# Gate projections moved behind the projections, and six PSUM banks for the first mixer, in a two-layer hybrid decoder on one core

## The chip, the cores and the metric

The kernel runs on one core of a Trainium2 chip. The metric is device time in microseconds for one execution, the median of three runs. The core's engines are TensorE (PE, with its weight loads PEld), VectorE (DVE), ScalarE (ACT), GpSimd (POOL) and SyncE (SP), which here only issues DMAs.

## The reference

2048 positions of width 1024 pass through a gated short-convolution mixer and then a stick-breaking attention of 8 heads of width 64, all in float32. Keys and values come from one shared projection.

```python
h = _rmsnorm(x, norm_a)                                   # layer 0: mixer
b_gate, c_gate, xin, g = jnp.split(h @ w_in, 4, axis=-1)
y = b_gate * _causal_depthwise_conv(c_gate * xin, w_conv)
x = x + (y * jax.nn.silu(g)) @ w_out
k, v = jnp.split(_rmsnorm(x, norm_kv) @ w_kv, 2, axis=-1) # shared
q, g = jnp.split(_rmsnorm(x, norm_b) @ w_in_b, 2, axis=-1)  # layer 1
z = jnp.einsum("bhqd,bhkd->bhqk", q, k) * HEAD_DIM ** -0.5
rev = lax.cumsum(where(mask, log_sigmoid(-z), 0.0), axis=3, reverse=True)
o = einsum("bhqk,bhkd->bhqd", exp(where(mask, z + rev, -inf)), v)
x = x + (o * jax.nn.silu(g)) @ w_out_b
return _rmsnorm(x, norm_f)
```

## The kernel before

Everything is held transposed: 128 channels on the partitions, positions along the free axis. The 2048 positions are cut into four chunks of 512 (in reversed order, so that the reversed cumulative sum becomes a forward scan). Each float32 product is made of three TensorE products: both operands are split into a high part in fp32r and a remainder (`split`: ACT makes the high part, DVE or POOL the remainder), and `mm3` (lines 202 to 214) runs high x high, high x low, low x high. A block of 128 output channels over 1024 input channels is therefore 24 matmuls of 512 columns. Weights are split once, kept in DRAM with their two halves, and loaded by SP for every later use, 1 MB for each block, into four buffers (`whl`).

The work for one chunk `c`:

- `mixer_in` (line 282): for each of 8 channel blocks the four parts C, X, B and G of the input projection, 24 matmuls each, followed by convolution and gating on DVE and ACT; the result goes to `y_d` in DRAM. Chunks 0 and 1 run together and share each weight load; chunks 2 and 3 run alone.
- `proj_out` (line 372): the mixer's output projection (8 blocks, tiles `po`), the residual, the norm, and the split normed tiles `xn`, kept in SBUF in `kept[c]`.
- `proj_k`, `proj_q`, `proj_v`, `proj_g`: 4 blocks each. The gate block (`proj_g`, tiles `pg` and `sgb`) ends with a sigmoid on ACT, a product on DVE and a write to `sg_d`. `proj_first` holds the output projection and the first k, q and v block, `proj_rest` the others and all four gate blocks.
- `attention` (line 466) for one head: for each chunk of keys up to `c`, four tiles of scores `z`, two sigmoids on ACT, a scan on DVE (line 501), a product (line 505), then transposes on TensorE (`wt`), a split (`wth` on ACT, `wtl` on DVE), and the product with the values into `av`. A head ends with the addition into `ot` (line 531).
- `out_b` (line 567): attention output times gate (`gated`), the last output projection (8 blocks of 12 matmuls, tiles `pob`), residual, sum of squares; `out_stat` and `out_norm` finish the last norm. For chunk 3 `out_b_last` does this in two parts, three quarters before the last pair of heads is done and the rest at the end.

PSUM has eight banks of one 128x512 tile: two each for `lin` (all projections), `z` and `wt`, one for `av`, one for `st` (norm statistics). A projection's bank is free again when DVE or ACT has read it.

What is issued next is decided in two steps. The program is made of generators that yield their cost, and `merge` (line 672) runs several of them side by side, always the one that has the smallest share of its stated total done; the totals are counted in `LIN`, one block of 24 matmuls (`TA` a mixer chunk, `TF` and `TR` the first and the remaining projections, `TO` an output projection). A scheduler then places the instructions on each engine's queue in that order of priority. Within a queue the order is fixed. SP's queue is one: a load stands behind an earlier write that still waits for its data.

The merges before are, in order: the mixer of chunks 0 and 1; the projections of chunk 0 with part of chunk 2's mixer; the projections of chunk 1 with more of that and attention of chunk 0; the rest of chunk 2's mixer with attention of chunk 1; the projections of chunk 2 with chunk 3's mixer and attention; the rest of that mixer with attention of chunk 2; `proj_first(3)` with the rest of attention of chunk 2; then these:

```python
fill = chain(proj_rest(3), gated_in(0), out_b(0, range(KD)), out_stat(0), gated_in(1), ...
merge((fill, TR + 3 * TO), (heads(0, 3, 3), 0.75 * ta(3)))
tail = chain(gated_in(3, range(3)), take(last, NB * 9 * MM), out_norm(2), until(last, -1.0))
merge((tail, 72 * MM), (heads(3, 4, 3), 0.25 * ta(3), S7))
```

In these last two the filler is paced: every third matmul of a projection is ordered behind the ninth last product of attention with the values.

Of the kernel before, what the change touches and what calls it, by code (L numbers as in the profile page):

```python
# [8 lines left out]
F32 = mybir.dt.float32  # L9
# [5 lines left out]
P = 128  # L15
# [3 lines left out]
KD = D // P  # L19
# [26 lines left out]
def kernel(  # L46
# [47 lines left out]
    k_d = [[dram.tile([P, CH], F32, name=f"k_d_{c}_{h}") for h in range(NH)] for c in range(NCH)]  # L94
    q_d = [[dram.tile([P, 2, CH], F32, name=f"q_d_{c}_{h}") for h in range(NH // 2)] for c in range(NCH)]
    v_d = [dram.tile([P, 4, NH, 2, 64], F32, name=f"v_d_{c}") for c in range(NCH)]
    sg_d = [[dram.tile([P, CH], F32, name=f"sg_d_{c}_{h}") for h in range(NH // 2)] for c in range(NCH)]
    og_d = [[dram.tile([P, CH], F32, name=f"og_d_{c}_{h}") for h in range(NH // 2)] for c in range(NCH)]

# [177 lines left out]
        return hc  # L277

    h = {}
    late_acc, late = {}, {}  # L280

    def mixer_in(cs):
# [3 lines left out]
        for cb in range(KD):  # L286
            wts = {}
            for c in cs:
# [5 lines left out]
                def gate(g, i):  # L294
                    if c not in h:
                        if c == 0:
                            load_first = lambda: wts.update({g: load_w(w_src(i), (g, cb), f"{g}{cb}_{cs[0]}")})
                            h[c], late_acc[c] = norm_x_late(c, load_first)
                        else:
                            h[c], xs = norm_x_late(c)  # L300
                            late_acc[c] = rstd(squares(c, xs), f"h{c}")
                    if g not in wts:
                        wts[g] = load_w(w_src(i), (g, cb), f"{g}{cb}_{cs[0]}")
                    if c == cb == 0 and g in "BG":

                        ps = psum.tile([P, CH], F32, name=f"p{g}_{nm}", tag="z", bufs=NZ)
                    else:
                        ps = lin(f"p{g}_{nm}")
                    yield from mm3(ps, wts[g], h[c])
                    return ps  # L310
# [61 lines left out]
    def proj_out(c):  # L372
# [23 lines left out]
        for k in range(KD):  # L396
            xn = act_tile(f"xn_{c}", k)
            nc.vector.tensor_mul(x1[k], x1[k], pb)
            split(xn[:, 0, :], xn[:, 1, :], x1[k], nc.gpsimd if k in XNL else nc.vector)
            kept[c].append(xn)  # L400
        yield YP[c] * 24 * MM

    def proj_k(c, kb):
# [49 lines left out]
    def proj_rest(c):  # L453
        yield from proj_k(c, 1)
        yield from proj_q(c, 1)
        yield from proj_v(c, 1)
        yield from proj_v(c, 2)
        yield from proj_v(c, 3)
        for i in (2, 3):
            yield from proj_k(c, i)  # L460
            yield from proj_q(c, i)
        for i in range(4):
            yield from proj_g(c, i)

# [198 lines left out]
    def take(g, cost):  # L663

        while cost > 0:
# [3 lines left out]
            cost -= r  # L669
            yield r  # L670

    def merge(*streams):

        anchors.clear()
# [8 lines left out]

    UD, UF = 3300.0, 5300.0
    LIN = 24 * MM
    TA, TF, TR, TO = 32 * LIN, 11 * LIN, 13 * LIN, 4 * LIN

    def ta(c):
        return 8 * UD + 8 * c * UF
# [4 lines left out]
    def heads(lo, hi, c):  # L694
        for hb in range(lo, hi):
# [5 lines left out]
            else:  # L701
                nc.sync.dma_start(out=og_d[c][hb], in_=ot)

    TP = TF + TR
    m01 = mixer_in((0, 1))
    run(take(m01, TA / 4))
    merge((m01, 1.75 * TA), (chain(iter((DLY,)), stats_x(2), stats_x(3), fold_gains()), 18.0 + DLY))
# [5 lines left out]
    m3 = mixer_in((3,))  # L713
    merge((chain(proj_first(2), proj_rest(2)), TP), (take(m3, F3 * TA), F3 * TA), (a1, (1 - F2) * ta(1), S3))
    merge((m3, (1 - F3) * TA), (take(a2, F4 * ta(2)), F4 * ta(2), S4))
    merge((proj_first(3), TF), (a2, (1 - F4) * ta(2)))
    fine[:] = [GRY, True]
    lo, hi = range(0, NB), range(NB, KD)
    fill = chain(proj_rest(3), gated_in(0), out_b(0, range(KD)), out_stat(0), gated_in(1),
                 out_b(1, lo), out_norm(0), out_b(1, hi), gated_in(2), out_stat(1),  # L720
                 out_b(2, lo), out_norm(1), out_b(2, hi), out_stat(2))
    merge((fill, TR + 3 * TO), (heads(0, 3, 3), 0.75 * ta(3)))
    tail = chain(gated_in(3, range(3)), take(last, NB * 9 * MM), out_norm(2), until(last, -1.0))
    merge((tail, 72 * MM), (heads(3, 4, 3), 0.25 * ta(3), S7))
    run(last)


# [25 lines left out]
```

## Time and profile before

| | |
|---|---|
| median of 3 runs | 1899.47 us (1899.46 to 1902.62) |
| profiled execution | 1899.87 us, span 1898.2 us |
| PE busy | 1787.5 us (94%), 8312 matmuls |
| DVE busy | 1264.4 us (67%) |
| ACT busy | 771.9 us (41%) |
| POOL busy | 433.3 us (23%) |
| mean granted TensorE clock | 0.975 |
| DMA | 443.65 MB, mean 234 GB/s |

Busy time is an average over stages with different limits, and a matmul that waits counts as busy. So the profile is read by stage: windows of the span with each engine's busy time, and the times at which heads end.

### The profile page before, as it was taken

To read this page: it belongs to the slowest core of one execution; us is meant where nothing else is said; L and a number is where in the kernel's file an instruction comes from. 1 tells how busy PE (TensorE), PEld (TensorE's weight loads), DVE (VectorE), ACT (ScalarE), POOL (GpSimd) and SP (SyncE) were. 2 spreads that over 40 slices of the span, in tenths; PEclk is the share of its full clock that TensorE was granted. 3 is DMA by queue.
4 is the path that set the end of the run, shared out by engine and by line. 5 is a ranking of instruction groups with operands and counts; after the bars stand their busy time and mean duration, and the time that the engine had idled before them with its cause. 6 is when DMAs were issued, how large, how long until landed. Compare 5 with 4: busy or idle time off the path is not lost.

```text
span 1898.2 us, 24937 instructions
## 1 busy us (share of the span) xinstructions
PE 1787.5 (94%) x8312; PEld 1453.6 (77%) x8312; DVE 1264.4 (67%) x1927; ACT 771.9 (41%) x1497; POOL 433.3 (23%) x822
## 2 busy tenths in 40 slices
PE   7999999999999999999999999999989999888784
PEld 5777888888888878888888888888857777766563
DVE  7766533564133273538886437787996989999996
ACT  6323211231122132325453324444564666566553
POOL 5100000101011031202222102223231323654651
PEclk9999999999999999999999999999989999999797
DMA  9989855697888778776767776656838565777751
GB/s 291 313 293 311 301 154 163 198 355 252 292 270 283 225 261 266 243 266 204 266 214 264 236 253 202 202 191 197 253 104 266 178 195 175 251 252 252 236 170 50
DMA packets 233871, 443.65 MB, mean 234 GB/s; under 512 B 17936, under 2 KB 132624, under 8 KB 209168
## 3 DMA queue, kind: packets, MB, share of 16 engines
q1 hardware_dynamic: 173664, 383.31, 60.1%
q10 hardware_dynamic: 59920, 58.74, 10.7%
q8 instruction: 66, 1.08, 0.2%
q14 instruction: 61, 0.50, 0.1%
q0 software_dynamic: 160, 0.02, 0.1%
HBM read 314.34 MB, written 127.66 MB: 233 GB/s over the span
## 4 chain that ended last, share of the span: by engine, by line
PE 68%; DVE 17%; DMA 6%; issue 5%; ACT 2%; POOL 1%; SPq 0%; ACTq 0%; POOLq 0%; DVEq 0%
PE pX L208 8%; PE pB L208 7%; PE po L208 7%; PE pC L208 7%; PE pG L208 7%; DVE R L501 5%; PE pv L208 4%; PE pk L208 4%; PE wt L513 4%; PE pq L208 4%; PE pg L208 4%; DVE w L505 3%; PE av L523 3%; DVE wtl L175 2%; PE av L522 2%
## 5 line engine op out<-in xcount | busy, mean ns | idle before, releaser
L501 DVE TENSOR_TENSOR_SCAN R<-R,R,ones 128x512 f32<-128x512 f32 x192 | 259.2, 1352 | 23.5 <-ACT R L490 23.2
L490 ACT ACTIVATE R<-z 128x512 f32<-128x512 f32 (+1 forms) x320 | 174.2, 545 | 171.5 <-DVE R L501 80.5
L175 DVE TENSOR_TENSOR wtl<-wt,wth 128x512 fp32r<-128x512 f32 (+1 forms) x320 | 186.2, 600 | 60.7 <-ACT wth L174 60.1
L174 ACT CAST wth<-wt 128x512 fp32r<-128x512 f32 (+1 forms) x320 | 160.6, 528 | 153.2 <-PE wt L513 134.1
L505 DVE TENSOR_TENSOR w<-w,R 128x512 f32<-128x512 f32 (+1 forms) x320 | 209.2, 661 | 16.1 <-POOL R L500 0.5
L208 PE MATMUL pC<-h,whl_C 128*128 128x512 f32 x768 | 193.3, 401 | 14.4 <-ACT whl_C L174 8.2
L208 PE MATMUL pX<-h,whl_X 128*128 128x512 f32 x768 | 188.4, 395 | 5.9 <-DVE cv L350 5.9
L208 PE MATMUL po<-y,whl_o 128*128 128x512 f32 x768 | 187.8, 392 | 0.0
L208 PE MATMUL pB<-h,whl_B 128*128 128x512 f32 x768 | 185.5, 391 | 0.0
L208 PE MATMUL pG<-h,whl_G 128*128 128x512 f32 x768 | 185.0, 391 | 0.0
L500 POOL COPY R<-R 128x1 f32<-128x1 f32 x192 | 103.9, 541 | 349.3 <-DVE R L501 302.2
L208 PEld LDWEIGHTS pC<-h,whl_C 128*128 128x128 f32 x768 | 146.4, 193 | 48.5 <-ACT whl_C L174 8.2
L513 PE MATMUL wt<-ident,w 128*128 128x128 f32 x1088 | 178.5, 279 | 4.3 <-DVE w L505 3.2
L492 ACT ACTIVATE w<-z 128x512 f32<-128x512 f32 (+1 forms) x320 | 171.9, 542 | 6.5 <-PE wt L513 6.5
L208 PEld LDWEIGHTS pX<-h,whl_X 128*128 128x128 f32 x768 | 143.9, 189 | 37.3 <-issue 3.6
L523 PE MATMUL av<-wtl,vv 128*128 128x512 f32 (+1 forms) x320 | 128.9, 405 | 41.5 <-DVE wtl L175 40.1
L208 PEld LDWEIGHTS po<-y,whl_o 128*128 128x128 f32 x768 | 143.1, 188 | 30.2 <-ACT y L174 0.4
L208 PEld LDWEIGHTS pB<-h,whl_B 128*128 128x128 f32 x768 | 143.4, 188 | 29.6
L208 PEld LDWEIGHTS pG<-h,whl_G 128*128 128x128 f32 x768 | 143.3, 188 | 29.7 <-DVE sgb L443 0.2
L513 PEld LDWEIGHTS wt<-ident,w 128*128 128x128 f32 x1088 | 139.7, 144 | 33.1 <-issue 4.2
L501 DVE TENSOR_TENSOR_SCAN R<-R,ones 128x512 f32<-128x512 f32 (+3 forms) x128 | 116.8, 918 | 36.0 <-POOL R L496 32.5
L487 PE MATMUL z<-kt,q 128*128 128x512 f32 (+1 forms) x320 | 129.9, 408 | 7.3 <-ACT w L492 7.1
(170 smaller groups left out, 2676.9 us busy)
## 6 DMA issues: line engine op xcount, KB each, us to landing
whl_o<-sw_o SPq DMA_DIRECT2D x24, 1024.0 KB, 6.1
kt<-k_d ACTq DMA_DIRECT2D x80, 256.0 KB, 4.0
vv<-v_d ACTq DMA_DIRECT2D x80, 256.0 KB, 4.2
whl_C<-sw_C SPq DMA_DIRECT2D x16, 1024.0 KB, 5.9
whl_X<-sw_X SPq DMA_DIRECT2D x16, 1024.0 KB, 5.4
whl_B<-sw_B SPq DMA_DIRECT2D x16, 1024.0 KB, 5.5
whl_G<-sw_G SPq DMA_DIRECT2D x16, 1024.0 KB, 5.3
whl_k<-sw_kv SPq DMA_DIRECT2D x16, 1024.0 KB, 5.6
```

The lines of the kernel that those rows point to most:

```text
L174: nc.scalar.copy(hi, src)
L175: eng.tensor_sub(lo, src, hi.bitcast(F32))
L208: ins = nc.tensor.matmul(ps, w[:, k, :], a[k][:, m, :], start=n == 0, stop=n == 3 * kt - 1)
L487: nc.tensor.matmul(ps[:, lom:CH], q2[:, 0, qi * P:(qi + 1) * P], kt[:, lom:CH], start=True, stop=False)
L490: nc.scalar.activation(R[:, lo + 1:CH + 1], ps[:, lo:CH], AF.Sigmoid, scale=-0.125)
L492: nc.scalar.activation(w[:, lo:CH], ps[:, lo:CH], AF.Sigmoid, scale=0.125)
L500: nc.gpsimd.tensor_copy(R[:, 0:1], carry[qi])
L501: nc.vector.tensor_tensor_scan(out=R[:, lo + 1:CH + 1], data0=R[:, lo + 1:CH + 1], data1=ones[:, 0:1].to_broadcast([P, CH - lo]), initial= ...
L505: nc.vector.tensor_mul(w[:, lo:CH], w[:, lo:CH], R[:, lo:CH])
L513: nc.tensor.transpose(wt[:, qi * P:(qi + 1) * P], ws[qi][:, kb * P:(kb + 1) * P], ident)
L522: nc.tensor.matmul(av[:, 0:n], vs, wh[:, 0:n], start=first, stop=False)
L523: ins = nc.tensor.matmul(av[:, 0:n], vs, wl[:, 0:n], start=False, stop=final)
```

## The change

The gate projections are taken out of `proj_rest`. Chunk 2's run beside chunk 3's output projection and attention of chunk 2; chunk 3's, and then those of chunks 0 and 1, run as filler beside attention of chunk 3, chunk 1's in turn with chunk 0's last output projection. For chunks 0 and 1 the normed tiles `xn` are by then gone from SBUF, so they are written to DRAM (`xn_d`, 8 tiles of 512 KB per chunk) and loaded again as `xa`. The last output projection of chunk 2 moves from the filler of the first three pairs of heads to that of the last pair. The mixer's results for chunks 0 and 1 go in turn to the two banks each of `lin`, `z` and `wt`, in place of `lin` with two exceptions.

```diff
+    xn_d = [[dram.tile([P, 2, CH], F32, name=f"xn_d_{c}_{k}") for k in range(KD)] for c in range(NCH - 2)]
...
+    turn = [0]
...
-                    if c == cb == 0 and g in "BG":
-
-                        ps = psum.tile([P, CH], F32, name=f"p{g}_{nm}", tag="z", bufs=NZ)
+                    if len(cs) > 1:
+
+                        tag, bufs = (("lin", NLIN), ("z", NZ), ("wt", NWT))[turn[0] % 3]
+                        turn[0] += 1
+                        ps = psum.tile([P, CH], F32, name=f"p{g}_{nm}", tag=tag, bufs=bufs)
...
             kept[c].append(xn)
+            if c < NCH - 2:
+                nc.sync.dma_start(out=xn_d[c][k], in_=xn.bitcast(F32))
...
         for i in (2, 3):
             yield from proj_k(c, i)
             yield from proj_q(c, i)
+
+    def proj_gate(c, again=True):
+        if again:
+
+            kept[c] = [act_tile(f"xa_{c}", k) for k in range(KD)]
+            for k in range(KD):
+                nc.sync.dma_start(out=kept[c][k].bitcast(F32), in_=xn_d[c][k])
         for i in range(4):
             yield from proj_g(c, i)
...
+    def zipped(*gens):
+
+        live = list(gens)
+        while live:
+            for g in list(live):
+                r = next(g, None)
+                if r is None:
+                    live.remove(g)
+                else:
+                    yield r
...
-    TA, TF, TR, TO = 32 * LIN, 11 * LIN, 13 * LIN, 4 * LIN
+    TA, TF, TR, TG, TO = 32 * LIN, 11 * LIN, 13 * LIN, 4 * LIN, 4 * LIN
...
-    TP = TF + TR
+    TP = TF + TR - TG
...
-    merge((proj_first(3), TF), (a2, (1 - F4) * ta(2)))
+
+    merge((proj_first(3), TF), (a2, (1 - F4) * ta(2)), (proj_gate(2, False), TG))
...
-    fill = chain(proj_rest(3), gated_in(0), out_b(0, range(KD)), out_stat(0), gated_in(1),
-                 out_b(1, lo), out_norm(0), out_b(1, hi), gated_in(2), out_stat(1),
-                 out_b(2, lo), out_norm(1), out_b(2, hi), out_stat(2))
-    merge((fill, TR + 3 * TO), (heads(0, 3, 3), 0.75 * ta(3)))
-    tail = chain(gated_in(3, range(3)), take(last, NB * 9 * MM), out_norm(2), until(last, -1.0))
-    merge((tail, 72 * MM), (heads(3, 4, 3), 0.25 * ta(3), S7))
+    first_out = chain(gated_in(0), out_b(0, range(KD)), out_stat(0))
+    fill = chain(proj_rest(3), proj_gate(3, False), proj_gate(0), zipped(first_out, proj_gate(1)), gated_in(1),
+                 out_b(1, lo), out_norm(0), out_b(1, hi), gated_in(2), out_stat(1))
+    merge((fill, TR + 2 * TG + 2 * TO), (heads(0, 3, 3), 0.75 * ta(3)))
+    tail = chain(out_b(2, lo), out_norm(1), out_b(2, hi), out_stat(2),
+                 gated_in(3, range(3)), take(last, NB * 9 * MM), out_norm(2), until(last, -1.0))
+    merge((tail, TO + 72 * MM), (heads(3, 4, 3), 0.25 * ta(3), S7))
```

Three places show how the instructions move. In the rows below the first letters name the tile, the next figure its block, and the last number only tells tiles apart; `x3` is three such instructions.

On TensorE, at the end of chunk 0's projections, the last gate block (`pg_3`) stood ahead of chunk 1's output projection (`po_0`). Before:

```order
L208 MATMUL pg_3_4293<-xn_5_3526,whl_gg_3_4291 128x512 x3
L208 MATMUL pg_3_4293<-xn_6_3530,whl_gg_3_4291 128x512 x3
L208 MATMUL pg_3_4293<-xn_7_3534,whl_gg_3_4291 128x512 x3
L513 MATMUL wt_1_0_2_4837<-ident,w_1_0_2_4737 128x128
L208 MATMUL po_0_4365<-y_0_4322,whl_o_0_4363 128x512
```

Now the last query block (`pq_3`) stands there:

```order
L209 MATMUL pq_3_4193<-xn_5_3579,whl_q_3_4191 128x512 x3
L209 MATMUL pq_3_4193<-xn_6_3584,whl_q_3_4191 128x512 x3
L209 MATMUL pq_3_4193<-xn_7_3589,whl_q_3_4191 128x512 x3
L535 MATMUL av_1_4565<-wth_1_0_1_4750,vv_1_0_4568 128x256
L536 MATMUL av_1_4565<-wtl_1_0_1_4751,vv_1_0_4568 128x256
L535 MATMUL av_1_4565<-wth_1_0_0_4758,vv_1_0_4568 128x256
L209 MATMUL po_0_4265<-y_0_4222,whl_o_0_4263 128x512
```

The four gate blocks are gone from this place, and likewise at the end of the projections of chunks 1 and 2.

On SP's queue, where chunk 0's normed tiles are made, the weights of the first key block (`whl_k_0`) and of the mixer's next blocks were followed by loads of the residual (`x_1`). Before:

```order
L194 DMA whl_k_0_3694<-sw_kv_1297 128x2048
L389 DMA x_1_0_4390<-in_xT_dram 128x512
L389 DMA x_1_1_4519<-in_xT_dram 128x512
L389 DMA x_1_2_4603<-in_xT_dram 128x512
L194 DMA whl_C_2_3728<-sw_C_0_980 128x2048
```

Now:

```order
L406 DMA xn_d_0_203<-xn_0_3554 128x1024
L393 DMA x_1_0_4290<-in_xT_dram 128x512
L406 DMA xn_d_3_206<-xn_3_3569 128x1024
L393 DMA x_1_1_4419<-in_xT_dram 128x512
L195 DMA whl_k_0_3778<-sw_kv_1313 128x2048
L406 DMA xn_d_1_204<-xn_1_3559 128x1024
L406 DMA xn_d_6_209<-xn_6_3584 128x1024
L406 DMA xn_d_2_205<-xn_2_3564 128x1024
L406 DMA xn_d_4_207<-xn_4_3574 128x1024
L406 DMA xn_d_5_208<-xn_5_3579 128x1024
```

The writes of `xn` stand among the weight loads, two of them ahead of the first key block's, and each waits for its tile's split.

On TensorE in chunk 3's third head (head 2, tiles `z_2`, `wt_2`, `av_2`), the filler between attention's matmuls was the last of chunk 3's gates and then chunk 0's output projection. Now chunk 0's gates on the reloaded tiles `xa` stand there:

```order
L209 MATMUL pg_3_14193<-xn_7_12474,whl_gg_3_14191 128x512 x3
L209 MATMUL pg_0_14298<-xa_0_14280,whl_gg_0_14296 128x512
L500 MATMUL z_2_0_0_14270<-kt_2_0_14266,q_3_2_13877 128x512
L501 MATMUL z_2_0_0_14270<-kt_2_0_14266,q_3_2_13877 128x512
L209 MATMUL pg_0_14298<-xa_0_14280,whl_gg_0_14296 128x512
L535 MATMUL av_2_13880<-wth_2_2_3_14067,vv_2_2_14008 128x512
L209 MATMUL pg_0_14298<-xa_0_14280,whl_gg_0_14296 128x512
L209 MATMUL pg_0_14298<-xa_1_14281,whl_gg_0_14296 128x512 x3
L209 MATMUL pg_0_14298<-xa_2_14282,whl_gg_0_14296 128x512 x3
L536 MATMUL av_2_13880<-wtl_2_2_3_14068,vv_2_2_14008 128x512
```

Eight gate blocks of 24 matmuls that ran in the projections of chunks 0 and 1 now lie between the matmuls of these heads.

## The prediction

> **What bounds the kernel now.** I read the page's 40 slices first, to see which engine is full where. Each digit is the busy share of 47 us, in tenths.
>
> ```profile
> PE   7999999999999999999999999999989999888784
> DVE  7766533564133273538886437787996989999996
> PEclk9999999999999999999999999999989999999797
> DMA  9989855697888778776767776656838565777751
> ```
>
> TensorE is full for two thirds of the span while VectorE is half idle. From slice 33 on it is the other way round: VectorE reads 9 throughout, and TensorE drops to 8 and 7. So a TensorE job is worth its full length early and perhaps little late. The windows by stage give the sizes (the columns are named in the first row).
>
> ```profile
> core 0: us, PE busy (x) PEld busy (x) DVE busy (x) ACT busy (x) POOL busy (x), PEclk, DMA share, GB/s
> 69.00:237.00 168.00, 162.15 (x697) 133.01 (x698) 101.73 (x163) 43.94 (x65) 6.70 (x15) 0.97 0.87 296
> 237.00:386.00 149.00, 149.00 (x659) 123.35 (x658) 64.58 (x82) 33.05 (x43) 9.06 (x16) 1.00 0.58 179
> 386.00:588.00 202.00, 201.28 (x912) 166.31 (x911) 79.92 (x139) 46.57 (x84) 15.24 (x35) 1.00 0.86 290
> 588.00:842.00 254.00, 251.41 (x1184) 208.94 (x1183) 111.50 (x196) 69.24 (x155) 41.32 (x116) 1.00 0.77 255
> 842.00:1144.00 302.00, 300.76 (x1465) 249.96 (x1464) 198.54 (x315) 123.80 (x258) 55.69 (x152) 1.00 0.72 240
> 1144.00:1313.00 169.00, 169.00 (x845) 141.08 (x843) 134.44 (x182) 81.71 (x169) 46.32 (x100) 1.00 0.60 192
> 1313.00:1475.00 162.00, 147.63 (x699) 115.88 (x697) 135.14 (x207) 85.67 (x178) 43.11 (x94) 0.96 0.66 213
> 1475.00:1614.00 139.00, 132.98 (x666) 108.77 (x667) 126.84 (x165) 85.93 (x173) 44.72 (x87) 0.98 0.57 180
> 1614.00:1831.00 217.00, 179.70 (x816) 136.72 (x815) 207.52 (x299) 128.18 (x255) 120.66 (x158) 0.92 0.73 236
> 1831.00:1867.00 36.00, 28.68 (x130) 21.57 (x129) 30.82 (x41) 19.26 (x37) 13.38 (x16) 0.91 0.36 114
> ```
>
> From 386 to 1313 TensorE is busy 922 of 927 us: every matmul taken out there ends the stage earlier. From 1614 to 1867 VectorE is busy 238 of 253 us.
>
> A busy TensorE also counts waiting inside a matmul, so I count its work instead: one block of 24 matmuls of 512 columns, and one transpose.
>
> ```profile
> 565.21 5.44 PE pg L208 x24
> ```
> ```profile
> 1461.99 0.82 PE L513 MATMUL wt<-ident,w 128*128 128x128 f32 x6
> 1462.56 0.48 PE L487 MATMUL z<-kt,q 128*128 128x512 f32 x1
> 1462.88 0.40 PE L488 MATMUL z<-kt,q 128*128 128x512 f32 x1
> ```
>
> A block takes 5.44 us, so a matmul 0.227 us; six transposes and one z make 0.89 us start to start, so a transpose 0.11 us. Adding TensorE's order at these prices gives 1697 us of work, the same before and after: the change only moves it. The span is 1898.2 us; about 200 us of it TensorE works at nothing. The change can only win by shrinking those 200.
>
> To see where the late ones lie I cut the trace at the ends of attention heads, the last addition into `ot` (start us, us, engine and line).
>
> ```profile
> 1313.20 0.69 DVE L531 TENSOR_TENSOR ot<-ot,av 64x512 f32<-64x512 f32 x1
> ...
> 1475.03 0.69 DVE L531 TENSOR_TENSOR ot<-ot,av 64x512 f32<-64x512 f32 x1
> ...
> 1614.18 0.67 DVE L531 TENSOR_TENSOR ot<-ot,av 64x512 f32<-64x512 f32 x1
> ...
> 1831.54 0.67 DVE L531 TENSOR_TENSOR ot<-ot,av 64x512 f32<-64x512 f32 x1
> ...
> 1867.07 0.69 DVE L531 TENSOR_TENSOR ot<-ot,av 64x512 f32<-64x512 f32 x1 [1.21 <-ACT ot L530]
> ```
>
> **Term 1, gates out of the full stages.** Four gate blocks leave each of chunks 0, 1 and 2: 3 x 4 x 5.44 = 65.3 us. In TensorE's order the work ahead of the end of the twentieth head (1313.20) falls from 1260 to 1190 us, 70.5: the other 5 us are blocks that the new merge weights put later. The stages they leave are TensorE's, so all of it counts: **-70.5 us**. With each gate block go a sigmoid of 0.60 us and a product of 0.69.
>
> ```profile
> L443 DVE TENSOR_TENSOR sgb<-sgb,pg 128x512 f32<-128x512 f32 x16 | 11.0, 685 | 44.8 <-ACT sgb L442 44.8
> ...
> L442 ACT ACTIVATE sgb<-pg 128x512 f32<-128x512 f32 x16 | 9.6, 598 | 41.8 <-PE pg L208 41.8
> ```
>
> They hid beside TensorE there. What is late next in those stages is the weight stream, term 3.
>
> **Term 2, six banks.** In the first mixer TensorE stops where a bank of `lin` still waits for VectorE (cv L339 reads pB, L350 reads pG).
>
> ```profile
> 68.98 8.25 PE L208 MATMUL pC<-h,whl_C 128*128 128x512 f32 x24 [3.11 <-DVE cv L339]
> 77.07 5.60 PE L208 MATMUL pX<-h,whl_X 128*128 128x512 f32 x24
> ...
> 124.90 7.34 PE L208 MATMUL pX<-h,whl_X 128*128 128x512 f32 x24 [3.20 <-DVE cv L350]
> ...
> 171.93 5.69 PE L208 MATMUL pX<-h,whl_X 128*128 128x512 f32 x24 [1.62 <-DVE cv L350]
> ...
> 216.74 5.72 PE L208 MATMUL pX<-h,whl_X 128*128 128x512 f32 x24 [1.04 <-DVE cv L350]
> ```
>
> The gaps are 3.11 + 3.20 + 1.62 + 1.04 = 9.0 us. The block behind the long ones runs slow (8.25 and 7.34 for 5.44), 5.2 us more: 14.2 in all. With six banks in turn TensorE may run six blocks, 33 us, ahead of VectorE, more than any of these gaps. What is late next is the weights, whose split passes through the same VectorE queue, at 87% DMA share. I take **-10 us**, bounds 0 and -14.2.
>
> **Term 3, the stored xn.** Sixteen writes of 512 KB are new, eight in each of chunks 0 and 1, on SP. Chunk 0's stage loses 4 MB of gate weights and gains 4 MB of writes, so its 0.86 x 202 = 174 us of DMA time now falls in about 180 us. No row shows these writes; the nearest are writes of the same size, the gate weights, and the busiest stretch beside the stretch where the writes will fall.
>
> ```profile
> q_d<-qhl SPq DMA_DIRECT2D x16, 512.0 KB, 4.5
> ```
> ```profile
> whl_gg<-sw_b SPq DMA_DIRECT2D x16, 1024.0 KB, 6.1
> ```
> ```profile
> 380.00:420.00 40.00, 40.00 (x178) 33.06 (x178) 26.23 (x43) 14.61 (x21) 0.00 (x0) 1.00 1.02 362
> 460.00:500.00 40.00, 39.32 (x176) 32.33 (x175) 12.20 (x18) 6.88 (x12) 4.74 (x6) 1.00 0.89 300
> ```
> ```profile
> 458.36 0.32 SPq L194 DMA_DIRECT2D whl_k<-sw_kv  x1
> ```
>
> At 362 GB/s 4 MB take 11.6 us. A weight load (whl_k at 458.36) is issued as one of four buffers comes free, so three blocks or 16 us before use, and lands in 5 or 6: 10 us of delay are covered. Behind the waiting writes on SP stand whl_k of block 0, the mixer's whl_B, then whl_q and whl_v; TensorE waits for them once the cover is used. Bounds: 0 with that cover in both chunks; 14 us if chunk 0, whose stage is already at 0.89 there, has none (11.6) and chunk 1 has it (some 2). I take a small stall: **+4 us**. A gain is excluded: nothing is issued earlier for it.
>
> **Term 4, the last twelve heads.** They take the 65 us back, with chunk 2's last output projection shifted from heads 3 to 6 into the last one. Per head I count TensorE's work and VectorE's, a 512-wide pass at 0.68 us and a scan at 1.28 us, the durations that these have undisturbed.
>
> ```profile
> L501 DVE TENSOR_TENSOR_SCAN R<-R,ones 128x512 f32<-128x512 f32 x32 | 41.1, 1284 | 6.3 <-POOL R L496 6.0
> ...
> L175 DVE TENSOR_TENSOR wtl<-wt,wth 128x512 fp32r<-128x512 f32 x224 | 149.2, 681 | 44.7 <-ACT wth L174 44.3
> ```
>
> Sums by group of heads; "larger" adds up the larger of the two, head by head:
>
> | heads | before: PE, DVE, larger, time | ratio | after: PE, DVE, larger |
> |---|---|---|---|
> | chunk 2, 4 to 7 | 131, 145, 160, 161.8 | 1.01 | 143, 140, 149 |
> | chunk 3, 0 to 2 | 125, 132, 132.5, 139.2 | 1.05 | 153, 143, 152.5 |
> | chunk 3, 3 to 6 | 150, 197, 197, 217.4 | 1.10 | 163, 189, 188.5 |
> | chunk 3, 7 | 24, 31, 31, 35.5 | 1.15 | 42, 47, 46.6 |
>
> TensorE's work grows by 70.5, but where VectorE was the larger that is free: the larger ones grow only from 521 to 537. With each group's own ratio the twelve heads take 572 instead of 554, +18. But heads in which both engines have nearly equal work do worse than either: the three such heads before took 1.08 to 1.10 of the larger (43.3 and 43.0 gave 46.6 us). After, most of the first seven are of that kind; 1.09 for those two groups gives 590, +36. I take the middle, **+27 us**. Bounds: VectorE's work alone sets the time, 518 x 554/505 = 568, +14; and 1.12 throughout, 601, +47.
>
> VectorE does slow down in heads 3 to 6.
>
> ```profile
> L501 DVE TENSOR_TENSOR_SCAN R<-R,R,ones 128x512 f32<-128x512 f32 x48 | 71.9, 1499 | 0.3 <-ACT R L490 0.3
> L505 DVE TENSOR_TENSOR w<-w,R 128x512 f32<-128x512 f32 x52 | 47.1, 906 | 2.7
> ```
>
> A scan takes 1.50 and a product 0.91 there, beside POOL's 121 us of work. POOL's instructions are as many as before, so this stays, in other heads; it is in the 1.10.
>
> **Sum.** -70.5 - 10 + 4 + 27 = -49.5 us. The profiled execution took 1899.87 us (span 1898.2), 0.4 above the median of the runs, so **1850 us**.
>
> **A rule to weigh.** In the windows the granted clock is 1.00 to 1313 and 0.92 and 0.91 in the last heads, and the block behind the 3.11 us gap took 8.25 us. In the Trainium skill, "TensorE: Matmul & The Clock Gate", section "What's actually happening", the array runs at half rate by default and only sustained activity of about 3.4 us releases it. The trace agrees in kind. By that rule work that fills the late gaps speeds up the matmuls around it, and term 4 would come out nearer nothing, as in the first rival.
>
> **The rivals.**
> - *Late heads take the gates for nothing* (0.14). The filler keeps TensorE's clock at 1.00 and the ratio falls to 1.03: 537 x 1.03 = 553, term 4 about 0, the rest -76.5: 1823 us. For it: the granted 0.92. Against: VectorE bounds these heads, and its work does not shrink.
> - *Late heads absorb badly* (0.20). Filler ahead of attention in TensorE's queue starves VectorE; 1.13 to 1.16 throughout, term 4 +53 to +69, say 61: 1884 us. For it: the last head's 1.15.
> - *Chunk 0's stage becomes the DMA's.* 14 us in term 3 in place of 4, the rest as forecast: 1860 us. It lies within the forecast's own spread and chance.
> - *Slower than before* (0.05). The queue starvation at its worst: in a head with half as much TensorE work again (chunk 3, head 0: 61 us for 40) each z waits behind a paced group and VectorE idles in turn. Term 1 is eaten once the ratio reaches (554 + 70.5) / 537 = 1.163; at 1.18, without the banks' gain and with 14 us of DMA stall, the sum is -70.5 + 14 + 80 = +23: 1923 us. Against: no group is above 1.15.
> - *Nothing happens* (0.03): ratios just at break-even, or the early stages bound by weights after all.
>
> **How the numbers follow.** The forecast, 1836 to 1870, has 0.58. The range takes in most of the first two rivals: **1826 to 1882**. A measurement here tells about 0.2%, 4 us, from no change. Faster 0.92, same 0.03, slower 0.05.
>
> **What would show it.** The twentieth head should end at 1313 - 77 = 1236 us; much later means term 1 or 3 is wrong, and then TensorE's waits at chunk 0's first k and q blocks name weights. No wait of a mixer matmul on cv should be left before 386. The twelve heads should take about 581 us, at a granted clock nearer 1.00 than 0.92 and with both engines over 85% busy. The tail behind the last head stays at 31 us. The prediction is wrong if the gates cost the late heads more than half of what they free.

## The result, and the profile after

| | before | after |
|---|---|---|
| median | 1899.46 us (1897.79 to 1902.62, 5 runs) | 1885.88 us (1879.31 to 1891.14, 5 runs) |
| profiled execution | 1899.87 us, span 1898.2 | 1879.31 us, span 1877.6 |
| granted TensorE clock | 0.975 | 0.979 |

The ratio is 0.9927 (95% interval 0.9908 to 0.9946): the change gains 13.6 us, 0.7%, where 49.5 were forecast. The profiled execution is the fastest of the five, 6.6 us under their median; the account of the trace below is that execution's.

The 40 slices of the page after, 47 us each, in tenths:

```profile
PE   7999999999999999999999999999988998988783
DVE  7876534554243364478785478787858889889984
PEclk9999999999999999999999999999999999999896
DMA  9999865697978798867677766566586667778763
```

Before, VectorE read 9 from slice 33 almost to the end; now it is 8 and 9 mixed, and TensorE 8 and 9. Both are nearly full and neither is full. The first output projection after the mixer (`po`) shows where the banks' gain ends: TensorE's timeline before, then after (start us, us).

```profile
385.50 2.88 PE L208 MATMUL po<-y,whl_o 128*128 128x512 f32 x12
```
```profile
369.26 5.61 PE L209 MATMUL po<-y,whl_o 128*128 128x512 f32 x24
```

The last additions into `ot` after, on VectorE's timeline, end heads 20, 24, 25 and 32 (they answer to L531 of before):

```profile
1237.81 0.69 DVE L544 TENSOR_TENSOR ot<-ot,av 64x512 f32<-64x512 f32 x1
...
1394.52 0.69 DVE L544 TENSOR_TENSOR ot<-ot,av 64x512 f32<-64x512 f32 x1 [0.61 <-ACT ot L543]
1470.09 0.67 DVE L544 TENSOR_TENSOR ot<-ot,av 64x512 f32<-64x512 f32 x1
...
1842.76 0.69 DVE L544 TENSOR_TENSOR ot<-ot,av 64x512 f32<-64x512 f32 x1 [5.65 <-ACT ot L543]
```

From these rows comes the whole account, as differences of starts:

| stretch | before | after | change | forecast |
|---|---|---|---|---|
| to the first `po` | 385.5 | 369.3 | -16.2 | -10 |
| `po` to the 20th head | 927.7 | 868.6 | -59.1 | -66.5 (terms 1 and 3) |
| the last twelve heads | 553.9 | 605.0 | +51.1 | +27 |
| behind the last head | 31.1 | 34.8 | +3.7 | 0 |
| sum | 1898.2 | 1877.6 | -20.6 | -49.5 |

What the gates free ahead of the 20th head is close to the forecast; the last twelve heads give almost all of it back. The windows of after show where (one row a head; the columns as in the prediction's first windows): head 24, head 25 (the first of chunk 3), and the last one, with the sum over all twelve.

```profile
1357.20:1394.50 37.30, 33.39 (x145) 25.60 (x146) 28.82 (x52) 17.84 (x35) 13.12 (x13) 0.91 0.76 284
1394.50:1470.10 75.60, 67.35 (x326) 53.80 (x325) 52.73 (x72) 36.58 (x77) 18.44 (x39) 0.98 0.66 211
...
1780.40:1842.80 62.40, 49.38 (x219) 37.83 (x218) 48.39 (x78) 29.52 (x54) 28.97 (x29) 0.91 0.69 214
sum 605.00, PE 545.44 PEld 435.44 DVE 511.33 ACT 330.49 POOL 237.44; mean PE 45.45 PEld 36.29 DVE 42.61 ACT 27.54 POOL 19.79
```

The sum over the same heads before:

```profile
sum 553.90, PE 488.79 PEld 382.74 DVE 500.23 ACT 318.90 POOL 221.86; mean PE 244.40 PEld 191.37 DVE 250.11 ACT 159.45 POOL 110.93
```

VectorE works 11 us more, 8 of them for twelve more gate products, and is idle 605.0 - 511.3 = 93.7 us where it was idle 53.7. In the last head neither engine is busy 80% of the time.

### The profile page after: what moved, and what is told of

It is laid out like the page before. It is cut to its first block, busy times and chain, and to the rows that moved or that the text cites. A ratio compares the mean times of both kernels' runs of the same rounds, so it can differ in the third digit from the quotient of the medians.

```text
span 1877.6 us, 24951 instructions
## 1 busy us (share of the span) xinstructions
PE 1771.9 (94%) x8312; PEld 1447.6 (77%) x8312; DVE 1261.9 (67%) x1927; ACT 772.7 (41%) x1497; POOL 450.4 (24%) x822
## 4 chain that ended last, share of the span: by engine, by line
PE 74%; DVE 10%; DMA 7%; issue 4%; ACT 2%; POOL 2%; SPq 0%; ACTq 0%; POOLq 0%; DVEq 0%
PE pX L209 9%; PE pB L209 9%; PE po L209 9%; PE pG L209 9%; PE pC L209 8%; PE wt L526 4%; PE pv L209 4%; PE pk L209 3%; PE pq L209 3%; DVE R L514 3%; PE pg L209 3%; PE av L536 3%; PE av L535 2%; PE z L500 2%; PE z L501 2%
## 5 line engine op out<-in xcount | busy, mean ns | idle before, releaser
L514 DVE TENSOR_TENSOR_SCAN R<-R,R,ones 128x512 f32<-128x512 f32 x192 | 255.0, 1330 | 25.2 <-ACT R L503 24.7
L513 POOL COPY R<-R 128x1 f32<-128x1 f32 x192 | 117.4, 613 | 340.9 <-DVE R L514 308.6
```

The lines of the kernel that those rows point to most:

```text
L513: nc.gpsimd.tensor_copy(R[:, 0:1], carry[qi])
L514: nc.vector.tensor_tensor_scan(out=R[:, lo + 1:CH + 1], data0=R[:, lo + 1:CH + 1], data1=ones[:, 0:1].to_broadcast([P, CH - lo]), initial= ...
```

## The experiments

Sixteen kernels ran. Beside each ratio stands its 95% interval; the runs of the kernel before that each was compared with had medians of 1898.93 to 1900.18 us.

### The two parts alone

Before with the six banks only:

```diff
-                    if c == cb == 0 and g in "BG":
...
-                        ps = psum.tile([P, CH], F32, name=f"p{g}_{nm}", tag="z", bufs=NZ)
+                    if len(cs) > 1:
...
+                        tag, bufs = (("lin", NLIN), ("z", NZ), ("wt", NWT))[turn[0] % 3]
+                        turn[0] += 1
+                        ps = psum.tile([P, CH], F32, name=f"p{g}_{nm}", tag=tag, bufs=bufs)
```

> The kernel before with the six banks alone. The first output projection block starts at 369.3 us in the changed kernel and at 385.7 before; if the banks do that alone, this kernel takes 16 us less than before, about 1883, with its twelve last heads as before (554 us). The prediction's size was 10 us, about 1889. Rival: the gain in the first mixer is eaten later because weights or the split come late, then 1895 or more.

Measured: 1882.36 us, 0.9924 (0.99 to 0.9948). And after with the old rule for the banks (the same diff reversed):

> The changed kernel with the old bank rule: only the gates, the stored xn and the moved output projection. If the two parts add up, it takes 16 us more than the changed kernel, about 1899 to 1902, so no better than before: the gates gain nothing by themselves, since what the early stages save (59 us to the twentieth head) the last twelve heads (51 us more) and the end (4 us more) give back. Rival: the gates are worth 10 us or more and the banks less, then 1890 or less.

Measured: 1897.33 us, 0.9997 (0.9979 to 1.0014). So **the banks are the whole gain, and the deferred gates as the change has them gain nothing**. In their profiles, with the banks alone `po` starts at 369.28 as in after; with the gates alone the twelve last heads take 609.5 us.

### Where the filler stands

Two kernels shift filler among the late heads. The first puts chunk 2's last output projection back where it was, out of the last head:

```diff
+                 out_b(2, lo), out_norm(1), out_b(2, hi), out_stat(2))
-    merge((fill, TR + 2 * TG + 2 * TO), (heads(0, 3, 3), 0.75 * ta(3)))
+    merge((fill, TR + 2 * TG + 3 * TO), (heads(0, 3, 3), 0.75 * ta(3)))
```

> The changed kernel with chunk 2's last output projection back in the filler of the first three pairs of heads. Theory: the last head is long (62 us for 47 us of VectorE's work) because its filler is put behind attention at the very end, where no other head overlaps; with the projection back the last head falls to 36 to 42 us and earlier heads take some 16 us more, the kernel 6 to 12 us less than the changed one. Rival: both engines are simply full over all twelve heads, and the total stays within 4 us of the changed kernel.

Measured: 1885.72 us, 0.9933 (0.9913 to 0.9952), the rival's time. The last head falls from 62.3 to 41.4 us, and the others take it: heads 26 to 31 grow from 310.4 to 336.6, and the twelve come to 615.6. The second holds back the filler of head 25 by giving the heads an exponent of 1.3 in the merge:

```diff
-    merge((fill, TR + 2 * TG + 2 * TO), (heads(0, 3, 3), 0.75 * ta(3)))
+    merge((fill, TR + 2 * TG + 2 * TO), (heads(0, 3, 3), 0.75 * ta(3), 1.3))
```

> The changed kernel with attention of chunk 3 preferred at the start of its merge (an exponent of 1.3 on its share), which takes the first head's TensorE work from 61 to 47 us and hands the filler to later heads. Theory: the first head loses 14 us because filler runs before attention has anything for VectorE (VectorE is busy 53 of 76 us there); with attention first VectorE starts earlier, 75.6 falls to 60 or less, and the twelve heads together lose 5 to 12 us: about 1875. Rival: what the first head gains the later ones give back, within 4 us of the changed kernel.

Measured: 1886.65 us, 0.9925 (0.991 to 0.9939), the rival's again. Head 25 falls from 75.6 to 66.7 us and the twelve from 605.0 to 598.0, but the work behind the last head grows from 34.8 to 50.0. My theory after the first trace, that the filler is in the wrong heads, fell: both kernels took the time out of the head they aimed at, and the total stayed.

### The store and the reload of xn

The store alone, on the kernel before, read by nobody:

```diff
+            if c < NCH - 2:
+                nc.sync.dma_start(out=xn_d[c][k], in_=xn.bitcast(F32))
```

> The kernel before with the sixteen writes of xn added and nothing else (the written tiles are not read). Theory: the writes delay weight loads, as the changed kernel reached the twentieth head 11 us later than its TensorE work says; 8 to 12 us more than before, about 1908 to 1911, with TensorE idle in chunk 0's projections. The prediction had 4 us, 1903. Rival: the writes are hidden, within 2 us of before, and the 11 us come from elsewhere.

Measured: 1902.34 us, 1.0017 (1.0004 to 1.0031), 3.4 us more than before, so near the prediction's 4 and not the 8 to 12 of the theory. Then after without the reload, first with the store and then without it too. These two compute the gates of chunks 0 and 1 from chunk 3's normed tiles, so their result is not the reference's; the amount of work is the same.

```diff
-            kept[c] = [act_tile(f"xa_{c}", k) for k in range(KD)]
-            for k in range(KD):
-                nc.sync.dma_start(out=kept[c][k].bitcast(F32), in_=xn_d[c][k])
+            kept[c] = kept[3]
```

> The changed kernel with the xn stores but without the reload (gates of chunks 0 and 1 are computed from chunk 3's normed tiles, so they are not the reference's). It splits the 22 us between the changed kernel and the one without store and reload. Theory: the stores cost 3 us, as on the kernel before, so about 1867; the reload 18. Rival: stores and reload each move 8.4 MB and cost alike, about 1874.

Measured: 1867.47 us, 0.9834 (0.982 to 0.9848), the theory's time.

> The changed kernel without the stored and reloaded xn: the gates of chunks 0 and 1 are computed from chunk 3's normed tiles in the same places, so the gates of these two chunks are not the reference's, while TensorE's, VectorE's and ScalarE's work stays the same and 16.8 MB of DMA go. Theory (balance): the late heads pay because TensorE and VectorE take turns at being the longer one; without the reload the kernel gains only the store's 3 to 6 us, 1880 to 1883. Rival (reload): the burst of loads on SP's queue at the start of chunk 3's heads and the DMA load at its fourth head make the 15 us lost before the twentieth head and the 15 us lost in the first head of chunk 3; then 15 to 30 us less than the changed kernel, 1856 to 1871.

Measured: 1863.36 us, 0.9802 (0.979 to 0.9815), inside the rival's 1856 to 1871; the theory of balance, 1880 to 1883, fell. By the medians the writes cost 1867.47 - 1863.36 = 4.1 us, and **the reload 1885.88 - 1867.47 = 18.4 us**. Against the banks alone, gates that need neither gain 1882.36 - 1863.36 = 19.0 us, and the two transfers take back 22.5. The two kernels without the reload also need no buffers for `xa` (16 of them, `NA`, serve all such tiles), so the 18.4 is the price of the loads together with the buffers that they hold. Another queue for the loads does not help:

```diff
-                nc.sync.dma_start(out=kept[c][k].bitcast(F32), in_=xn_d[c][k])
+                nc.scalar.dma_start(out=kept[c][k].bitcast(F32), in_=xn_d[c][k])
```

> The changed kernel with the reload of xn issued on ScalarE's queue in place of SP's. Rival (the burst on SP delays weight loads and the writes of k, q and v): the first head of chunk 3 falls from 75.6 us towards its 61 us of TensorE work, 8 to 12 us less in all, about 1875. Theory (balance): within 4 us of the changed kernel.

Measured: 1887.73 us, 0.9929 (0.9915 to 0.9944). The Trainium skill, "DMA: Bandwidth & Descriptors", section "Issuing engines are not separate DMA queues", says that transfers issued from any engine end on the same 16 DMA engines and that another issuer saves only issue time; this run agrees, with 1887.73 us for 1885.88. Last, after with the gates of chunks 0 and 1 back in their own stages, so that no xn is stored and only the gates of chunks 2 and 3 are later than before:

```diff
-    merge((chain(proj_first(0), proj_rest(0)), TP), (take(m2, F0 * TA), F0 * TA))
+    merge((chain(proj_first(0), proj_rest(0), proj_gate(0, False)), TP + TG), (take(m2, F0 * TA), F0 * TA))
...
-    fill = chain(proj_rest(3), proj_gate(3, False), proj_gate(0), zipped(first_out, proj_gate(1)), gated_in(1),
+    fill = chain(proj_rest(3), proj_gate(3, False), first_out, gated_in(1),
```

> The changed kernel with the gates of chunks 0 and 1 back at the end of their own projections (so no stored xn); chunk 2's and 3's stay deferred, the banks and the shifted output projection stay. Theory (balance): deferring the 43.5 us of gates of chunks 0 and 1 gains nothing, so this is within 5 us of the changed kernel and of the banks alone, 1880 to 1888. Rival: the deferral itself is worth what it frees in the early stages and something else (chunk 2's gates, the shifted projection) spoils the late heads; then this kernel is 10 us or more away from the changed one, slower if the deferral pays, faster if it costs.

Measured: 1882.83 us, 0.9907 (0.9893 to 0.9922): the banks' time again, as the theory had it.

### How the reload costs

Eight loads `xa` (chunk 0's) and eight loads `x` are issued within 15 us, ahead of the first writes of k (SP's timeline of after).

```profile
1367.27 1.89 SPq L629 DMA_DIRECT2D x<-x_d  x2
1369.21 4.35 SPq L474 DMA_DIRECT2D xa<-xn_d  x8
1375.50 5.36 SPq L629 DMA_DIRECT2D x<-x_d  x6
1381.83 0.32 SPq L195 DMA_DIRECT2D whl_q<-sw_b  x1
1383.09 2.38 SPq L417 DMA_DIRECT2D k_d<-khl  x4
```

The product that first uses them comes 159 us later (the gate products in the trace of after: count, least, median and longest ns, first and last start):

```profile
L209 PE MATMUL pg<-xa,whl_gg x192: 387/394/497, 1527.8 to 1651.6; 128*128 128x512 f32 x192
```

The windows of after around the burst, and those of the kernel with neither store nor reload, in which head 24 ends 4 us later:

```profile
1380.00:1400.00 20.00, 19.54 (x97) 15.37 (x95) 6.73 (x11) 5.26 (x11) 0.02 (x1) 1.00 0.96 365
1400.00:1420.00 20.00, 14.36 (x58) 11.16 (x58) 6.41 (x8) 4.50 (x12) 4.37 (x9) 0.91 0.81 257
```
```profile
1380.00:1400.00 20.00, 20.00 (x102) 16.39 (x100) 6.28 (x10) 5.66 (x10) 0.00 (x0) 1.00 0.99 318
1400.00:1420.00 20.00, 17.99 (x87) 13.88 (x87) 14.14 (x21) 10.37 (x24) 7.20 (x15) 1.00 0.70 235
```

In the first 20 us VectorE has little to do in both; with the reload it stays so for 20 us more. ScalarE's timeline of after says by what:

```profile
1392.51 0.59 ACT L175 CAST qhl<-pq 128x512 fp32r<-128x512 f32 x1
...
1399.79 0.58 ACT L175 CAST vt<-pvt 128x512 fp32r<-128x512 f32 x1 [5.30 <-DMA q_d<-qhl]
1399.81 2.84 ACTq L485 DMA_DIRECT2D q<-q_d  x4
...
1410.91 0.58 ACT L175 CAST khl<-pk 128x512 fp32r<-128x512 f32 x1 [10.54 <-DMA v_d<-vt]
...
1411.60 0.60 ACT L503 ACTIVATE R<-z 128x512 f32<-128x512 f32 x1
```

`khl`, `qhl` and `vt` share one buffer (`hl`, line 412 of after). The cast into it waits until the write of the one before to DRAM has landed, and behind these casts on ScalarE's queue stand the loads of q and the first sigmoids of head 25. The waits are there without the reload too, only shorter. The same places in the kernel with the stores and without the reload:

```profile
1380.92 2.38 SPq L417 DMA_DIRECT2D k_d<-khl  x4
```
```profile
1388.61 0.58 ACT L175 CAST qhl<-pq 128x512 fp32r<-128x512 f32 x1 [5.81 <-DMA k_d<-khl]
...
1394.44 0.59 ACT L175 CAST vt<-pvt 128x512 fp32r<-128x512 f32 x1
...
1404.50 0.59 ACT L175 CAST khl<-pk 128x512 fp32r<-128x512 f32 x1 [4.89 <-DMA v_d<-vt]
...
1405.19 0.60 ACT L501 ACTIVATE R<-z 128x512 f32<-128x512 f32 x1
```

With the reload the writes of k are issued 2.2 us later, behind the loads on SP's queue, and the writes of q and v take longer to land (DMA issues from 1360 to 1420, first of after, then without the reload; the last column is us to landing, the median):

```profile
q_d<-qhl SPq DMA_DIRECT2D x2, 512.0 KB, 5.5
v_d<-vt SPq DMA_DIRECT2D x1, 512.0 KB, 9.1
```
```profile
q_d<-qhl SPq DMA_DIRECT2D x2, 512.0 KB, 3.5
v_d<-vt SPq DMA_DIRECT2D x1, 512.0 KB, 8.0
```

Together the first sigmoid of head 25 starts 6.4 us later, and the head ends 7.6 later (1470.1 for 1462.5); 0.7 of each was there at the 20th head. So this chain covers at most 7 of the 14.1 us by which the two traces differ.

To test the chain, five kernels. The reload spread over the heads, each load ordered behind a later product with the values:

```diff
+                ld = nc.sync.dma_start(out=kept[c][k].bitcast(F32), in_=xn_d[c][k])
+                if len(anchors) > 20:
+                    tc.add_manual_dep(ld.ins, anchors[k - 21].ins.name, PACE, reason="pace")
```

> The changed kernel with each reload of xn ordered behind a product of attention with the values some 14 to 21 back, so chunk 0's eight loads fall between its gates' weights in the third head of chunk 3 and no longer at the start of the first. Theory (burst): the loads cost most where they meet the writes of k, q and v, whose single buffer then holds up ScalarE; head 24 and the first head of chunk 3 together fall from 113 to 106 us as without the reload, and the kernel takes 6 to 10 us less than the changed one, 1876 to 1880. Rival (total traffic): the 16.8 MB cost about 20 us wherever they lie; then within 4 us of the changed kernel.

Measured: 1881.27 us, 0.9905 (0.9892 to 0.9917), 4.6 less than after by the medians, between the theory and the rival; its four runs lie within the range of after's five, so the size is not settled. The trace shows what was aimed at: heads 21 to 25 take 226.3 us, for 232.3 in after and 225.4 without the reload. But heads 26 to 31 take 316.8 for 310.4. Then two `hl` buffers, first with the room taken from the load buffers (`NL` 5 to 3), beside a control with that room taken and one `hl`:

```diff
-NR, NW, NT, NL, NWB, NRAW, NA, NWTS = 5, 8, 4, 5, 4, 2, 16, 2
+NR, NW, NT, NL, NWB, NRAW, NA, NWTS = 5, 8, 4, 3, 4, 2, 16, 2
...
-        hl = sb.tile([P, 2, CH], F32R, name=f"khl_{c}_{kb}", tag="hl", bufs=1)
+        hl = sb.tile([P, 2, CH], F32R, name=f"khl_{c}_{kb}", tag="hl", bufs=2)
```

> The changed kernel with two buffers for the split k, q and v tiles (one before) and, to make room, three buffers for the general loads in place of five. Theory (single buffer): ScalarE's waits of 10.5 and 5.3 us for the landing of v and q at the start of chunk 3's heads go, and its pair with one buffer and the same three load buffers is 6 to 10 us slower. Rival: the burst delays the weights all the same, the pair within 4 us.

> The control of the run with two buffers: the changed kernel with three load buffers in place of five and nothing else. Fewer load buffers may cost up to 10 us by themselves in the last output projections; 1885 to 1896.

Measured: 1889.49 us, 0.9947 (0.9935 to 0.9959), and the control 1909.59 us, 1.0053 (1.0035 to 1.0072). The second buffer is worth 20 us there, more than expected, but three load buffers cost more than that, also more than expected: behind the last head it takes 73.6 and 73.8 us to the end, for 34.8. So the same pair with four load buffers, the rest of the room coming from three small tiles (`ones`, `syh`, `syl`):

> The changed kernel with two buffers for the split k, q and v tiles, made room for by four general load buffers in place of five, one tile of ones in place of two and single buffers for two tiny norm tiles. Theory (single buffer): the reload costs 18 us because the landing of each k, q or v write, 5 to 10 us under the load, holds up ScalarE and with it the attention that should start; with two buffers the first head of chunk 3 falls from 75.6 to about 60 us and the kernel is 10 us or more faster than its control with one buffer, about 1872. Rival (TensorE and VectorE alternate as the longer one, the buffer matters little): within 5 us of its control.

> The control: the changed kernel with the same small buffers and a single buffer for the split k, q and v. One load buffer less may cost some of what two less did: 1886 to 1898.

Measured: 1883.14 us, 0.9923 (0.9902 to 0.9944) with two buffers, and 1890.59 us, 0.9954 (0.9939 to 0.9969) with one: **7.5 us for the second buffer**, between the theory's 10 and the rival's 5. ScalarE's timeline of each, at the same casts, with two buffers and then with one:

```profile
1385.22 0.59 ACT L175 CAST vt<-pvt 128x512 fp32r<-128x512 f32 x1
...
1391.88 0.59 ACT L175 CAST khl<-pk 128x512 fp32r<-128x512 f32 x1 [2.90 <-PE pk L209]
...
1402.18 0.60 ACT L503 ACTIVATE R<-z 128x512 f32<-128x512 f32 x1 [3.74 <-PE z L501]
```
```profile
1400.41 0.59 ACT L175 CAST vt<-pvt 128x512 fp32r<-128x512 f32 x1
...
1412.08 0.58 ACT L175 CAST khl<-pk 128x512 fp32r<-128x512 f32 x1 [11.09 <-DMA v_d<-vt]
1412.71 0.60 ACT L503 ACTIVATE R<-z 128x512 f32<-128x512 f32 x1
```

The wait on the write is gone, and head 25's sigmoids start 10 us earlier. But a lead of 9.0 us was there before any `xa` is loaded: with two buffers the 20th head already ends at 1229.6 us, for 1238.6 with one. It comes from chunk 0's projections, shown under term 1. Heads 21 to 25 add 4.8 us, and of these 13.8 the rest of the kernel gives back all but 2.3 in these two traces. So the 7.5 us can't be booked as the reload's. Last, both remedies together, and a control that has the banks and the two buffers but gates where they were before:

> Two buffers and the paced reload together on the changed kernel. The pacing alone gave 5 us; if both remove the same stall, this is within 3 us of two buffers alone; if the pacing also spares later heads, 3 to 6 us less.

> The kernel before with the six banks, and the same two buffers for k, q and v and the same smaller other buffers: the whole setting without the deferred gates. If the single buffer was what ate the gates' gain, this is 8 us or more slower than the same with deferred gates; if the late heads eat it anyway, the two are within 4 us.

Measured: both remedies **1874.78 us, 0.988 (0.9858 to 0.9901)**, the fastest kernel here with the whole computation; the control 1882.35 us, 0.9918 (0.9898 to 0.9938). Against two buffers alone the spreading gains 8.4 us, more than either branch expected. With the reload spread and two buffers, the deferred gates gain 7.6 us over the control; with two buffers alone (1883.14) still nothing, so the single buffer alone did not eat their gain.

## Why the prediction was wrong

It held that the late heads would give back two fifths of the saved 66.5 us, 27; they gave back 51 of 59. Two of its steps failed: term 3 gave the loads that bring the tiles back no price, and they cost 18.4 us; and term 4 was too small even without them, 38.9 us for 27. Term 1 missed a limit that took 9 us. Head by head (us; 32 with what lies behind it):

| | 20th ends | 21-24 | 25 | 26-31 | 32 and end |
|---|---|---|---|---|---|
| before | 1313.2 | 161.8 | 45.5 | 311.0 | 66.6 |
| banks alone | 1296.0 | 160.8 | 45.3 | 308.9 | 65.3 |
| after | 1237.8 | 156.7 | 75.6 | 310.4 | 97.2 |
| after, no store or reload | 1235.7 | 162.7 | 62.8 | 307.0 | 94.3 |
| after, two `hl`, four load buffers | 1229.6 | 165.7 | 62.7 | 323.5 | 100.2 |
| spread reload, two `hl` | 1229.1 | 167.8 | 55.9 | 318.0 | 98.7 |

**Term 2, six banks: the mechanism right, the size low.** -16.2 in the trace and 16.6 us by the medians, for -10. After, no wait of TensorE is left between 60 and 370. The four gaps and the slow blocks behind them came to 14.2, the upper bound; the 1.55 us that TensorE waited there for the norm's statistics (`pst_h`) went too. The weights, for which I held 4 us back, are not among its waits there.

**Term 1, gates out of the full stages: right, once a second limit is away.** Without store and reload `po` to the 20th head falls by 927.7 - 866.3 = 61.4 us, 9 short of 70.5. The term let TensorE run on without the gates, and named only the weights as what is late next. It was the single `hl` buffer. TensorE's busy time in chunk 0's projections in after, and with two buffers:

```profile
372.00:552.00 180.00, 174.91 (x782) 143.74 (x781) 76.31 (x130) 42.93 (x81) 17.95 (x48) 0.98 0.85 298
```
```profile
372.00:552.00 180.00, 178.43 (x809) 147.14 (x808) 74.28 (x125) 42.79 (x77) 14.95 (x35) 1.00 0.91 316
```

In after a split waits there for the landing of the write before it (ScalarE's timeline), and TensorE for that split, which reads its bank:

```profile
504.62 0.58 ACT L175 CAST khl<-pk 128x512 fp32r<-128x512 f32 x1 [7.49 <-DMA v_d<-vt]
```
```profile
505.99 5.77 PE L209 MATMUL pv<-xn,whl_v 128*128 128x512 f32 x24 [1.34 <-DVE khl L176]
```

With two buffers `po` to the 20th head takes 860.4 us, 67.3 less than before and with the stores in it, for a forecast of 66.5; its control with one buffer takes 869.4. With the gates in their old place the second buffer gains nothing there (928.4 us, for 926.7 with the banks alone), so it is the moved gates that bring this limit up.

**Term 3: the step that failed first.** It counted the sixteen writes, at +4, and they cost 3.4 and 4.1 us. It gave the sixteen loads that bring the tiles back no price at all, though the change lists them, and they cost 18.4 us. The loads are not late themselves: no product waits for an `xa` tile. They delay the writes of k, q and v, those hold the one `hl` buffer, and through ScalarE's queue head 25's first sigmoids wait. This chain is shown in the traces for at most 7 of the 14.1 us by which after and its pair without the reload differ there; these are the fastest executions of both, and the slower ones of after have no trace. The rest of the 18.4 stays open. One place is visible: chunk 1's loads are issued from 1581.0 on, the first product on them starts at 1588.8, and from 1567.4 on TensorE has no filler, where without the reload the next gate product follows within 2 us of the last of chunk 0. Head 28 is then 2.7 us shorter and head 29 6.9 longer; no run isolates this. The remedies, 1885.88 - 1874.78 = 11.1 us together, also remove term 1's waits, so they don't measure the chain.

**Term 4, the late heads: under-sized even without the reload.** +38.9 us in the twelve heads without store and reload, for +27, and 3 more behind them. The table places it: heads 26 to 31 take no more than with the banks alone, 307.0 for 308.9. Head 25 costs 17.5 us more and stands at its work: TensorE is busy 60.4 of its 62.8 us. So its price is filler that TensorE must do, and was forecast. The excess lies in two places. The first four heads, with TensorE's and VectorE's work nearly equal (143 and 140), took 162.7, 1.09 of the larger; the forecast's middle had 1.05. The last head, with chunk 2's output projection now in it, took 60.4 for 46.6 of work, 1.30, where I took 1.15. Putting that projection elsewhere did not help (615.6 us in twelve heads), so the cost is not of that place. I take it that two queues of fixed order, nearly equal in work, wait for each other in turn wherever the filler stands. That is argued from VectorE's idle time, 94 us in after for 54 before, part of which is the reload's; no run isolates it.

**The clock.** By the Trainium skill, "TensorE: Matmul & The Clock Gate", section "What's actually happening", the array is throttled by default and activity releases it. The prediction drew from it that work in the late gaps would speed up the matmuls. The granted clock in head 25 is 0.98, for 0.96 before and 1.00 without store and reload, but in the last head still 0.91, as before, though that head has more than half as much TensorE work again (42 us for 24). The rule is not refuted, since the array there was idle as often as before: 13 of 62.4 us for 7 of 36. The hope drawn from it fails in that head.

**The rivals and marks.** The nearest rival is "late heads absorb badly", whose 1884 us is 2 from the median. That is partly luck: it put the heads at 1.13 to 1.16 of the larger work throughout, and they took 605.0 / 537 = 1.13 with the reload but 592.8 / 537 = 1.10 without, so about a quarter of its price is the reload's (12.2 of 51.1 us); and the banks gave 6 us more than it counted. Of the marks, the 20th head at 1236 (1237.8) held, but by two errors that cancel, 6 us more from the banks and 7 less from the gates; the mixer's waits held. The twelve heads at 581 (605.0), a clock near 1.00 in the last of them and an unchanged tail (34.8 for 31) failed; TensorE was over 85% busy in them (545 of 605 us), VectorE just not (511). The named condition, that the gates cost the late heads more than half of what they free, came true.

## What to carry to other kernels

Moving work out of a stage that one engine fills gains its full length there only if no second limit is close: here a single buffer took 9 us of 70, and a second one gave them back. Where the work lands it must be priced as a sum of three: the work itself, the loss where two engines then have nearly equal work, and every transfer that the move itself needs, in both directions. A transfer is priced not only by who waits for its data but by whose buffer is held while it loads the DMA engines; a single buffer that is freed by a write's landing puts a DMA burst onto a compute queue. Of a change in two parts, run each alone before explaining the sum. And when a remedy helps, look where in the trace the gain begins: the second buffer was meant for the reload, and most of its lead arose 800 us ahead of it.

## What the runs showed of the hardware

- Writes of 512 KB land in very different times. Those of v took 4.6 us in the median of 16 in after, the one issued at 1401.1 us 9.1, with the DMA engines 0.88 busy at 279 GB/s; the same write took 8.0 without the reload. The sixteen of `xn` took 9.0 in the median.
- Runs of one kernel can lie 10 us apart without any change in the program: 1877.96 to 1888.13 with the banks alone, 1879.31 to 1891.14 in after, but 1880.55 to 1881.99 with the loads spread. Why was not found.
- Two load buffers fewer left the end of the last head where it was (1839.0 us for 1842.8) and cost 39 us behind it in the trace, its slowest execution; by the medians the cost is 1909.59 - 1885.88 = 23.7 us.
